# A convolution with residual add: the weights loaded as 16 rows of 9 KB, with four output channels each, and transposed in 36 pieces of 16 columns

## The chip, the cores and the metric

The kernel runs on one core of a Trainium2 chip. The metric is the device time of one execution in microseconds (us). Before the change it is 124.16 us, the median of three runs that lie between 124.1 and 124.16.

The core has the engines PE (matrix products), DVE (vector work), ACT (scalar work, here casts), POOL (here zeros and the identity) and SP (which only issues transfers here). Sixteen DMA engines, shared by all queues, move data between the chip's main memory (HBM) and the on-chip memory (SBUF). The results of PE land in PSUM, which DVE reads. Engines wait for each other through semaphores.

## The reference

A 3 x 3 convolution with padding 1 over 16 images of 64 channels and 64 x 64 pixels, into 64 channels, and then the addition of a residual. Everything is float32.

```python
batch, c_in, h, w, c_out, k = 16, 64, 64, 64, 64, 3
x_pad = np.pad(x, ((0, 0), (0, 0), (pad, pad), (pad, pad)), mode='constant')
for b in range(batch):
    for co in range(c_out):
        for ci in range(c_in):
            for kh in range(k):
                for kw in range(k):
                    output[b, co] += weight[co, ci, kh, kw] * x_pad[b, ci, kh:kh+h, kw:kw+w]
return (output + residual).astype(np.float32)
```

x, the residual and the output are 16.8 MB each, the weights 0.147 MB. All of it crosses the DMA engines once.

## The kernel before

**Transfers.** The images are taken in pairs: two images of 64 channels fill 128 partitions, and a row of a partition is one channel of 4096 pixels, 16 KB. There are eight pairs. SP issues, in this order, for each pair the load of x (`load_x`, line 71, into one of three buffers `xr`) and the load of the residual (`load_ro`, line 74, into a buffer `ro` of its own for each pair). The load of the very first pair of x is moved ahead of the barrier at the start of the program (`to_the_front`). From the fourth pair on, the load of x waits until ACT has read the buffer that it takes (line 123). Then come the stores (line 77): five in the same queue, each waiting for its pair's additions (line 129), and the last three after everything else is done (lines 217 and 218). All these transfers are in one queue, q1, and are worked off in the order of issue by all 16 DMA engines.

**The weights** are loaded by one DMA that ACT issues (line 151, queue q10) into `wraw`. Before the change this is a buffer of 64 partitions, one for each output channel, with a row of 576 float32 numbers (64 input channels times 9 taps), 2304 bytes. PE needs the weights with the input channels on the partitions. So PE waits for the zeros and the identity (line 191) and for the weights (line 192), and then turns the nine 64 x 64 blocks, one for each tap, with a transpose against a 64 x 64 identity (line 195), into the first bank of PSUM. DVE copies the nine blocks from there, cast to bfloat16, into the tile `wl` in six instructions (line 172). `wl` holds each tap in the two places where a 128 x 128 matrix of two output rows and two input rows needs it; the places that stay zero are set by POOL (lines 147 and 148).

**POOL** first makes the identity (a memset on line 133 and a select on line 135), then sets the border rows of the four `xp` buffers and the zero places of `wl`. Each of these counts `s_id` up.

**The loop over 16 images.** ACT casts the even and the odd rows of an image into the two halves of an `xp` buffer (lines 159 and 163). PE runs 24 matrix products of 128 x 128 by some 512 for each image, six weight tiles with four chunks each (lines 83 and 84). It starts the first image when `wl` is written (`s_bank`, line 199) and the image is cast (`s_pack`, line 200). DVE adds the residual to the two halves of the result, in place in `ro` (line 182), and that frees the store. The order on each engine is the order of the program.

Of the kernel before, what the change touches and what calls it, by code (L numbers as in the profile page):

```python
# [8 lines left out]
FP32 = mybir.dt.float32  # L9
# [6 lines left out]
def kernel(  # L16
# [7 lines left out]
    nc = tc.nc  # L24
# [18 lines left out]
    w_flat = weight.rearrange("co ci kh kw -> co (ci kh kw)")  # L43

    pool = ctx.enter_context(tc.tile_pool(name="pool", bufs=1))
    psum = ctx.enter_context(tc.tile_pool(name="psum", bufs=1, space=bass.MemoryType.PSUM))

    ident = pool.tile([64, 64], FP32)
    ro = [pool.tile([128, NPIX], FP32, name=f"ro{p}") for p in range(NPAIR)]
    xr = [nc.alloc_sbuf_tensor(f"xr{i}", [128, NPIX], FP32) for i in range(NXR)]  # L50

    xp = [pool.tile([128, J + 1, W], BF16, name=f"xp{i}") for i in range(NXP)]
    wraw = nc.alloc_sbuf_tensor("wraw", [64, 576], FP32)
    wl = pool.tile([128, 2, 3, 2, 64], BF16)
    ps = [psum.tile([128, NCHUNK, JC, W], FP32, name=f"ps{i}") for i in range(2)]

    sem = lambda name: tc.alloc_semaphore(name)
    s_w = sem("s_w")
# [11 lines left out]
    def load_x(p):  # L70
        return nc.sync.dma_start(out=xr[p % NXR][:, :], in_=x_bc[128 * p : 128 * p + 128, :]).then_inc(s_x[p % NXR], 16)

    def load_ro(p):
        nc.sync.dma_start(out=ro[p][:, :], in_=res_bc[128 * p : 128 * p + 128, :]).then_inc(s_r[p], 16)

    def store(p):
        return nc.sync.dma_start(out=out_bc[128 * p : 128 * p + 128, :], in_=ro[p][:, :])

    def matmul(out_, lhsT, rhs, start, stop, ldweights):

        e = nc.tensor
        if ldweights:
            return e.matmul(out=out_, lhsT=lhsT, rhs=rhs, start=start, stop=stop, skip_group_check=True)  # L83
        return e.add_instruction(  # L84
            mybir.InstMatmult(
                name=nc.get_next_instruction_name(),
                engine=PE,
                ins=[e.lower_ap(rhs), e.lower_ap(lhsT)],
                outs=[e.lower_ap(out_)],
                start_tensor_calc=start,  # L90
                stop_tensor_calc=stop,
                tile_size=(128, 128),
                tile_position=(0, 0),
                bass_skip_group_check=True,
                ldweights=False,
            )
        )

    def to_the_front(dma):

        def fixed(ap):
            t = ap.bass_ap.tensor.name
            return mybir.PhysicalAccessPattern(
                ap=ap.ap, offset=ap.bass_ap.offset, dtype=ap.dtype, memref=t, memsetref=t + "_set", bass_ap=ap.bass_ap
            )

        front = nc.main_func.blocks[0].instructions
        here = nc.cur_bb.bb.instructions  # L110
        ins = here.pop()
        assert ins.name == dma.ins.name
        at = next(
            i for i, e in enumerate(front) if e.engine == mybir.EngineType.SP and isinstance(e, mybir.InstDrain)
        )
        front.insert(at, copy.replace(ins, ins=[fixed(a) for a in ins.ins], outs=[fixed(a) for a in ins.outs]))

    with tc.tile_critical(no_gpsimd_drain=True):  # L118

        for p in range(NPAIR):  # L120
            if p >= NXR:

                nc.sync.wait_ge(s_half, 2 * (p - NXR) + 3)
            i = load_x(p)
            if p == 0:
                to_the_front(i)
            load_ro(p)
        for p in range(NEARLY):
            nc.sync.wait_ge(s_add, 2 * p + 3)
            store(p).then_inc(s_out, 16)  # L130


        nc.gpsimd.memset(ident[:, :], 0.0).then_inc(s_id, 1)  # L133
        nc.gpsimd.wait_ge(s_id, 1)
        nc.gpsimd.affine_select(  # L135
            out=ident[:, :],
            in_=ident[:, :],
            compare_op=mybir.AluOpType.not_equal,
            fill=1.0,
            base=0,  # L140
            pattern=[[-1, 64]],
            channel_multiplier=1,
        ).then_inc(s_id, 1)
        for t in xp:
            nc.gpsimd.memset(t[0:64, 0, :], 0.0).then_inc(s_id, 1)  # L145
            nc.gpsimd.memset(t[64:128, J, :], 0.0).then_inc(s_id, 1)  # L146
        nc.gpsimd.memset(wl[0:64, 0, :, 1, :], 0.0).then_inc(s_id, 1)  # L147
        nc.gpsimd.memset(wl[64:128, 1, :, 0, :], 0.0).then_inc(s_id, 1)  # L148


        nc.scalar.dma_start(out=wraw[:, :], in_=w_flat[:, :]).then_inc(s_w, 16)
        for n in range(B):
            p, im = divmod(n, 2)
            hp = slice(64 * im, 64 * im + 64)
            x4 = xr[p % NXR].rearrange("q (j two w) -> q j two w", two=2, w=W)
            t = xp[n % NXP]
            if im == 0:
                nc.scalar.wait_ge(s_x[p % NXR], 16 * (p // NXR + 1))
            i = nc.scalar.copy(out=t[64:128, 0:J, :], in_=x4[hp, :, 0, :])  # L159
            i.then_inc(s_half, 1)  # L160
            if n >= NXP:
                i._wait_ge(s_conv, n - NXP + 1)
            nc.scalar.copy(out=t[0:64, 1 : J + 1, :], in_=x4[hp, :, 1, :]).then_inc(s_pack, 1)  # L163


        nc.vector.wait_ge(s_wt, 1)
        tpf = ps[0].rearrange("p c j w -> p (c j) w")

        blocks = ((0, 0, 0, 0), (1, 0, 0, 1), (1, 0, 1, 0), (0, 1, 0, 2), (0, 1, 1, 1), (1, 1, 1, 2))
        for half, d, par, kh in blocks:  # L170
            hp = slice(64 * half, 64 * half + 64)
            i = nc.vector.tensor_copy(out=wl[hp, d, :, par, :], in_=tpf[0:64, 3 * kh : 3 * kh + 3, :])  # L172
        i.then_inc(s_bank, 2)
        for n in range(B):
            p, im = divmod(n, 2)
            hp = slice(64 * im, 64 * im + 64)
            o4 = ro[p].rearrange("q (j two w) -> q j two w", two=2, w=W)
            psj = ps[n % 2].rearrange("q c j w -> q (c j) w")
            if im == 0:
                nc.vector.wait_ge(s_r[p], 16)  # L180
            for par in range(2):
                i = nc.vector.tensor_tensor(  # L182
                    out=o4[hp, :, par, :], in0=psj[64 * par : 64 * par + 64, :, :], in1=o4[hp, :, par, :], op=ADD
                )
                if par == 0:
                    i._wait_ge(s_conv, n + 1)

                i.then_inc(s_add if par == 0 or n == B - 1 else s_bank, 1)


        nc.tensor.wait_ge(s_id, 4 + 2 * NXP)
        nc.tensor.wait_ge(s_w, 16)
        wraw3 = wraw.rearrange("p (ci t) -> p ci t", t=9)
        for t in range(9):
            i = nc.tensor.transpose(out=ps[0][0:64, t // 8, t % 8, :], in_=wraw3[:, :, t], identity=ident[:, :])  # L195
        i.then_inc(s_wt, 1)
        with nc.Fori(0, B // NXP, 1, engines=[PE]):
            for n in range(NXP):
                nc.tensor.wait_ge(s_bank, 1).then_inc(s_bank, -1)
                nc.tensor.wait_ge(s_pack, 1).then_inc(s_pack, -1)  # L200
                order = [(1, 0), (1, 1), (0, 0), (0, 1), (2, 0), (2, 1)]
                for i, (kw, d) in enumerate(order):
                    xlo, xhi = max(0, 1 - kw), min(W, W + 1 - kw)
                    for c in range(NCHUNK):
                        j0 = JC * c
                        m = matmul(
                            ps[n % 2][:, c, :, xlo:xhi],
                            wl[:, d, kw, :, :].rearrange("q r c -> q (r c)"),
                            xp[n][:, j0 + d : j0 + d + JC, xlo + kw - 1 : xhi + kw - 1],
                            i == 0,  # L210
                            i == len(order) - 1,
                            c == 0,
                        )
                m.then_inc(s_conv, 1)
# [36 lines left out]
```

## Time and profile before

| what | value |
|---|---|
| median time | 124.16 us |
| the profiled execution's own time | 124.16 us |
| its span, first to last instruction | 122.1 us |
| PE busy | 86.5 us (71%) |
| DVE busy | 75.2 us (62%) |
| ACT busy | 62.0 us (51%) |
| moved by DMA | 50.48 MB, mean 413 GB/s |
| queue q1 (loads and stores) | 97.8% of the 16 DMA engines' time |
| queue q10 (weights) | 0.4%, 80 packets |
| weights: issue to landing | 8.5 us |

In the profile, a line such as L195 is a line of the kernel; `wl<-ps` says which tile is written from which. A group of instructions is shown with its busy time, the mean duration of one, and what ended the idle time before it. A view of windows gives, for each stretch of time, the busy time of each engine and then the clock granted to PE, the share of the 16 DMA engines that was busy, and the rate that they moved. A share can be a little over 1 in a short window, because a packet is counted in the window where it starts. A timeline gives start, duration, engine, line and operation. SPq, ACTq and PEq are the sequencers of these engines, which issue DMAs and wait.

### The profile page before, as it was taken

How to read it: one execution, taken by the hardware profiler on the slowest of the kernel's cores; microseconds unless marked ns; L12 is line 12 of the kernel's file. 1: busy time of each engine (PE TensorE's matmuls, PEld its weight loads, DVE VectorE, ACT ScalarE, POOL GpSimd, SP SyncE). 2: the span in 40 equal slices, each digit the busy share in tenths (PEclk: the TensorE clock that was granted, in tenths of full speed). 3: DMA queues.
4: the chain of work that ended last, by engine and by line, in shares of the span. 5: the costliest groups of instructions: out<-in, count | busy, mean ns of one | idle time of the engine just before them, and what ended most of it. 6: DMA issues, size and time to landing. Idle time of an engine off the chain costs nothing.

```text
span 122.1 us, 729 instructions
## 1 busy us (share of the span) xinstructions
PE 86.5 (71%) x389; PEld 10.4 (9%) x105; DVE 75.2 (62%) x38; ACT 62.0 (51%) x33; POOL 2.2 (2%) x16
## 2 busy tenths in 40 slices
PE   0003799999999999999999999999999930000000
PEld 0003000101111010101010101111110100000000
DVE  0004101989889898898989889898798988000000
ACT  4009948966984993992994896699000000000000
POOL 5100000000000000000000000000000000000000
PEclk9999999999999999999999999999999999555555
DMA  6999999999999999999999999999999999999993
GB/s 182 408 348 429 429 429 429 429 424 429 429 429 424 429 429 429 429 429 429 429 429 419 429 429 424 429 429 429 435 435 435 429 429 429 435 435 429 429 429 140
DMA packets 3536, 50.48 MB, mean 413 GB/s; under 512 B 400, under 2 KB 400, under 8 KB 464
## 3 DMA queue, kind: packets, MB, share of 16 engines
q1 hardware_dynamic: 3456, 50.33, 97.8%
q10 hardware_dynamic: 80, 0.15, 0.4%
HBM read 33.70 MB, written 16.78 MB: 413 GB/s over the span
## 4 chain that ended last, share of the span: by engine, by line
PE 70%; DVEq 2%; DVE 2%; issue 0%
PE ps L84 53%; PE ps L83 17%; DVEq L118 2%; DVE ro L182 2%
## 5 line engine op out<-in xcount | busy, mean ns | idle before, releaser
L182 DVE TENSOR_TENSOR ro<-ps,ro 64x2048 f32<-64x2048 f32 x32 | 73.2, 2289 | 17.4 <-PE ps L84 16.9
L84 PE MATMUL ps<-xp,wl 128*128 128x504 bf16 (+1 forms) x288 | 79.9, 387 | 0.2
L159 ACT CAST xp<-xr 64x2048 bf16<-64x2048 f32 x16 | 30.3, 1896 | 21.3 <-DMA xr<-in_x_dram 21.1
L83 PE MATMUL ps<-xp,wl 128*128 128x504 bf16 (+1 forms) x92 | 35.6, 387 | 2.4 <-PEq L200 2.4
L163 ACT CAST xp<-xr 64x2048 bf16<-64x2048 f32 x16 | 30.4, 1897 | 0.4
L83 PEld LDWEIGHTS ps<-xp,wl 128*128 128x128 bf16 x96 | 9.5, 99 | 77.5 <-issue 77.5
L172 DVE CAST wl<-ps 64x192 bf16<-64x192 f32 x6 | 1.9, 347 | 10.9 <-PE ps L195 10.8
L195 PE MATMUL ps<-ident,wraw 64*64 64x64 f32 x9 | 1.1, 305 | 9.6 <-DMA wraw<-in_weight_dram 9.6
L159 ACT ACT_TABLE_LOAD x1 | 1.3, 1283 | 1.5 <-SPq L118 1.5
L195 PEld LDWEIGHTS ps<-ident,wraw 64*64 64x64 f32 x9 | 0.9, 163 | 9.6 <-issue 9.6
L146 POOL MEMSET xp<- 64x64 bf16 x4 | 0.6, 147 | 0.2
L145 POOL MEMSET xp<- 64x64 bf16 x4 | 0.6, 145 | 0.2
L148 POOL MEMSET wl<- 64x192 bf16 x1 | 0.3, 253 | 0.1
L147 POOL MEMSET wl<- 64x192 bf16 x1 | 0.3, 252 | 0.1
L135 POOL TENSOR_SCALAR_AFFINE_SELECT ident<-ident 64x64 f32<-64x64 f32 x1 | 0.2, 233 | 0.2 <-POOL ident L133 0.2
L133 POOL MEMSET ident<- 64x64 f32 x1 | 0.1, 145 | 0.5 <-SPq L118 0.5
L235 POOL MEMSET const-bfloat16-1.0<- 128x1 bf16 x1 | 0.1, 113 | 0.0
L235 POOL MEMSET const-uint8-127<- 128x1 uint8 x1 | 0.1, 112 | 0.0
L235 POOL MEMSET const-float32-1.0<- 128x1 f32 x1 | 0.1, 109 | 0.0
L235 POOL MEMSET const-float32-0.0<- 128x1 f32 x1 | 0.1, 104 | 0.2 <-issue 0.2
## 6 DMA issues: line engine op xcount, KB each, us to landing
xr<-in_x_dram SPq DMA_DIRECT2D x8, 2048.0 KB, 17.6
ro<-in_residual_dram SPq DMA_DIRECT2D x8, 2048.0 KB, 22.1
out_dram<-ro SPq DMA_DIRECT2D x8, 2048.0 KB, 28.7
wraw<-in_weight_dram ACTq DMA_DIRECT2D x1, 144.0 KB, 8.5
```

Source lines behind the costliest of these rows:

```text
L83: return e.matmul(out=out_, lhsT=lhsT, rhs=rhs, start=start, stop=stop, skip_group_check=True)
L84: return e.add_instruction(mybir.InstMatmult(name=nc.get_next_instruction_name(), engine=PE, ins=[e.lower_ap(rhs), e.lower_ap(lhsT)], outs ...
L118: with tc.tile_critical(no_gpsimd_drain=True):
L145: nc.gpsimd.memset(t[0:64, 0, :], 0.0).then_inc(s_id, 1)
L146: nc.gpsimd.memset(t[64:128, J, :], 0.0).then_inc(s_id, 1)
L147: nc.gpsimd.memset(wl[0:64, 0, :, 1, :], 0.0).then_inc(s_id, 1)
L159: i = nc.scalar.copy(out=t[64:128, 0:J, :], in_=x4[hp, :, 0, :])
L163: nc.scalar.copy(out=t[0:64, 1 : J + 1, :], in_=x4[hp, :, 1, :]).then_inc(s_pack, 1)
L172: i = nc.vector.tensor_copy(out=wl[hp, d, :, par, :], in_=tpf[0:64, 3 * kh : 3 * kh + 3, :])
L182: i = nc.vector.tensor_tensor(out=o4[hp, :, par, :], in0=psj[64 * par : 64 * par + 64, :, :], in1=o4[hp, :, par, :], op=ADD)
L195: i = nc.tensor.transpose(out=ps[0][0:64, t // 8, t % 8, :], in_=wraw3[:, :, t], identity=ident[:, :])
L235: nc = _bacc.Bacc("TRN2", target_bir_lowering=False, num_devices=1)
```

## The change

The same bytes of the weights are read as 16 rows of 9216 bytes: a row holds four output channels that follow each other in memory. `wraw` so has 16 partitions, and partition q holds the output channels 4q to 4q + 3. A transpose takes, for one tap t and one u from 0 to 3, the 16 x 64 block of the output channels 4q + u, and writes 64 x 16 into every fourth column of the block of that tap in PSUM. There are 36 of them in place of nine. The identity is 16 x 16. What lies in PSUM afterwards is the same, and DVE's six copies, PE's loop and everything else are as before.

```diff
-    ident = pool.tile([64, 64], FP32)
+    ident = pool.tile([16, 16], FP32)
...
-    wraw = nc.alloc_sbuf_tensor("wraw", [64, 576], FP32)
+    wraw = nc.alloc_sbuf_tensor("wraw", [16, 4, 576], FP32)
...
-            pattern=[[-1, 64]],
+            pattern=[[-1, 16]],
...
-        nc.scalar.dma_start(out=wraw[:, :], in_=w_flat[:, :]).then_inc(s_w, 16)
+        nc.scalar.dma_start(out=wraw[:, :, :], in_=w_flat.rearrange("(q u) f -> q u f", u=4)).then_inc(s_w, 16)
...
-        wraw3 = wraw.rearrange("p (ci t) -> p ci t", t=9)
+        wraw4 = wraw.rearrange("q u (ci t) -> q u t ci", t=9)
         for t in range(9):
-            i = nc.tensor.transpose(out=ps[0][0:64, t // 8, t % 8, :], in_=wraw3[:, :, t], identity=ident[:, :])
+            for u in range(4):
+                i = nc.tensor.transpose(
+                    out=ps[0].rearrange("p c j (q u) -> p (c j) u q", u=4)[0:64, t, u, :],
+                    in_=wraw4[:, u, t, :],
+                    identity=ident[:, :],
+                )
         i.then_inc(s_wt, 1)
```

## The prediction

> **What bounds the kernel now.** I read the page first, for the shares; then windows of the DMA, because the page shows it full; then the timeline of the first 14 us, where the change lies, and of the end. The span is 122.1 us, the profiled execution took 124.16 us, which is also the median of the three runs, so every sum below is made on 124.16 with 2.06 us lying around the span.
>
> Lines of the page:
>
> ```profile
> span 122.1 us, 729 instructions
> ...
> PE 86.5 (71%) x389; PEld 10.4 (9%) x105; DVE 75.2 (62%) x38; ACT 62.0 (51%) x33; POOL 2.2 (2%) x16
> ...
> DMA  6999999999999999999999999999999999999993
> ...
> q1 hardware_dynamic: 3456, 50.33, 97.8%
> q10 hardware_dynamic: 80, 0.15, 0.4%
> ```
>
> No engine is above 71%, but the 16 DMA engines are full from the second slice to the last but one: q1 alone (the loads and stores that SP issues) takes 97.8% of them. The bytes set the time: 50.48 MB at some 429 GB/s are 117.7 us. The chain that ended last names PE for 70%, since it follows semaphores and does not know that the queue behind the last stores is still full. So I ask of everything whether it delays the DMA stream, and of the compute chain only whether the last stores are issued late enough for the stream to run dry. q10 is the weight load: 80 packets, 0.15 MB.
>
> Windows of the DMA (the last two columns are the share of the 16 engines and GB/s):
>
> ```profile
> 5.00:6.25 1.25, 0.00 (x0) 0.00 (x0) 0.00 (x0) 0.00 (x0) 0.00 (x0) 1.00 1.12 441
> 6.25:8.65 2.40, 0.00 (x0) 0.00 (x0) 0.00 (x0) 0.00 (x0) 0.00 (x0) 1.00 0.97 323
> 8.65:12.00 3.35, 1.14 (x9) 0.93 (x9) 1.16 (x4) 3.08 (x2) 0.00 (x0) 1.00 1.00 425
> ...
> 30.00:100.00 70.00, 68.58 (x316) 7.70 (x79) 61.51 (x28) 44.08 (x24) 0.00 (x0) 1.00 1.01 429
> ```
>
> There is one weak stretch: from 6.25 to 8.65 us the engines are busy (0.97) and move only 323 GB/s; before and after it the rate is full. The packet records of the trace put the 64 weight packets of 2304 B at 5.2 to 8.3 us, so the stretch begins about 1 us after the first and ends 0.4 us after the last. The large packets running in it are longer too, on all 16 engines, also those whose weight packets are done.
>
> The start and the end, from the timeline and from windows:
>
> ```profile
> 0.95 0.53 ACTq L151 DMA_DIRECT2D wraw<-in_weight_dram  x1
> ...
> 9.60 0.93 PEld L195 LDWEIGHTS ps<-ident,wraw 64*64 64x64 f32 x9 [9.60 <-issue]
> 9.63 1.14 PE L195 MATMUL ps<-ident,wraw 64*64 64x64 f32 x9 [9.63 <-DMA wraw<-in_weight_dram]
> 10.81 1.97 DVE L172 CAST wl<-ps 64x192 bf16<-64x192 f32 x6 [10.81 <-PE ps L195]
> 10.81 1.90 ACT L163 CAST xp<-xr 64x2048 bf16<-64x2048 f32 x1
> ...
> 13.12 0.58 PE L83 MATMUL ps<-xp,wl 128*128 128x512 bf16 x1 [2.35 <-PEq L200]
> ```
>
> ```profile
> 98.78 4.61 DVE L182 TENSOR_TENSOR ro<-ps,ro 64x2048 f32<-64x2048 f32 x2 [0.58 <-PE ps L84]
> 103.68 1.76 SPq L77 DMA_DIRECT2D out_dram<-ro  x3
> ```
>
> ```profile
> 105.00:105.50 0.50, 0.00 (x0) 0.00 (x0) 0.00 (x0) 0.00 (x0) 0.00 (x0) 0.50 1.00 426
> 105.50:106.00 0.50, 0.00 (x0) 0.00 (x0) 0.00 (x0) 0.00 (x0) 0.00 (x0) 0.50 1.16 492
> ...
> 120.00:120.50 0.50, 0.00 (x0) 0.00 (x0) 0.00 (x0) 0.00 (x0) 0.00 (x0) 0.50 0.16 66
> ```
>
> Weights landed, nine transposes, six copies into wl: they end at 12.78 us. The casts of the first image end at 12.71. PE needs both and starts at 13.12; from there to 98.7 it has no gap. The last three stores are issued at 103.68. Their 6.29 MB take 14.6 us at 430 GB/s, and the DMA stops at about 120.1, so their bytes started at about 105.4, with no dip at 105 to 106. The very first load was issued at 0.00 and its bytes came from about 1.0 us on. The same latency would have let the stores begin at 104.7. So the compute chain may slip by about 0.7 us before the stream runs dry. Bounds of this cover: 0, if the latency is the whole 1.7 us, and 1.7 us.
>
> **The change part by part.**
>
> **POOL.** Identity of 16 x 16 in place of 64 x 64: the memset (0.14 us) and the select (0.23 us) can only shrink. POOL ends its zeros at 3.71 us and PE waits for the weights until 9.60, so this is worth nothing; the cover is 5.9 us.
>
> **Queues.** No wait is added and nothing is moved past a queue. SP's issues stay. ACT still issues one DMA (0.53 us) ahead of its table load, which ends at 2.80, and ACT then waits for x until 8.89. A shorter issue gains nothing, and one of twice the length is hidden.
>
> **The weight transfer** is what touches the bound. Now: over 5.00 to 8.65 us the windows give (1.25 x 441 + 2.40 x 323) / 3.65 = 363 GB/s against 429, which is 0.24 MB or 0.56 us lost; the weights' own 0.147 MB are 0.34 us. The load costs the stream 0.90 us today, 0.56 of it over its bytes. Afterwards the bytes are the same, in 16 rows that land in 16 partitions in place of 64. If the loss went with the number of packets, it would fall to a quarter: 0.14 + 0.34 = 0.48, a gain of 0.42 us; if nothing were lost, the gain is 0.56. If it goes with what each receiving partition has to take, it rises up to four times: 2.24 + 0.34 = 2.58, a loss of 1.68 us. I stand nearer to the second, because the slow stretch does not look like a price per packet: it starts late, ends late, and slows the x packets on every engine, like a backlog on the receiving side. Between none and four times I take twice: 1.12 + 0.34 = 1.46, that is +0.56 us. Both ends stay for the range.
>
> [...]
>
> **The transposes.** Nine at a pitch of (1.14 - 0.29) / 8 = 0.107 us become 36. Each still loads 64 columns as its stationary side; the moving side shrinks from 64 columns to 16. Bounds of the pitch: a quarter (0.027, 1.2 us in all with the 0.29 us tail) if the moving columns set it, and unchanged (0.107, 4.0 us) if the load does. I take between them 0.067, 2.6 us in all, against 1.14 now: +1.5 us.
>
> [...]
>
> Against this the weights may land earlier. One packet and one completion for each engine, instead of four packets with a large one between each two (about 0.7 to 0.9 us apart in the packet records), saves up to 2 us: 7.6 instead of 9.6. With the backlog that I expect, about 1 us: 8.6. Transposes end at 8.6 + 2.6 = 11.2, 0.4 us later than 10.77. The six copies and PE's start follow by as much: 13.5. This is inside the 0.7 us. Should it go well (7.6 + 1.2 = 8.8), the casts at 12.71 take over and PE starts 0.1 to 0.2 us earlier, worth nothing since the DMA sets the end.
>
> **Sum.** POOL 0, issue 0, transfer +0.56 (-0.56 to +1.68), transposes 0 behind the cover: 124.16 + 0.56 = 124.72, said as 124.7.
>
> **The rivals.**
>
> *Per-packet cost (faster).* A quarter of the packets means a quarter of the loss: -0.42, 123.74; down to 123.6 if nothing is lost. For it: packets of 2304 B are the only small data packets in the trace, and the weak stretch lies where they are. Against it: the first of them ran at 0.093 us each with the rate still full (441 GB/s at 5.00 to 6.25). It decides if the loss follows packets, not partitions.
>
> *No difference.* The weak stretch has another cause (first reads of the residual tensor come in the same microseconds), or the AP is still cut into pieces of 2304 B and the change does not do what it says, or the two effects cancel: 124.0 to 124.4. Against the first: no other start of a load shows a weak stretch.
>
> *PE becomes late (slower).* If the weights land at 9.6 as now and the pitch stays 0.107, the transposes end at 13.6, 2.9 us later; less the 0.7 of cover, 2.2 us of idle DMA: 126.4. It decides from an end of the transposes after about 11.5 us. Against it: fewer packets cannot well land later than now unless the backlog is severe, and the moving side is a quarter.
>
> **How the numbers follow.** A measurement of this kernel can tell about 0.2% (0.25 us) from no change. Transfer dearer, my forecast: 0.45, with loss factors 1.5 to 3, so 124.4 to 125.3. PE late: 0.10, 125.0 to 126.4. No difference: 0.18. Faster: 0.27, 123.6 to 123.9. So slower 0.55, same 0.18, faster 0.27. The range 123.65 to 125.25 leaves out most of the late PE, and little of the ends of the other two, some 0.15 in all.
>
> **What would show it.** Right: q10 with 32 packets; a window between 5 and 9 us with the engines busy and a rate below 323 GB/s, or as weak for longer; the last three stores' bytes without a dip, the DMA ending near 120.7. The landing of wraw near 7.5 us after its issue; transposes of 2 to 3 us. Wrong: the rate between 6 and 9 us near 400, and a DMA that ends before 119.9 (per-packet cost); a window below 400 GB/s between 104 and 108 us (PE late).

## The result and the profile after

The changed kernel takes 125.87 us (median of six runs, 125.14 to 126.04) against 124.18 us before (124.1 to 124.43, six runs). The ratio is 1.0123 with an interval of 1.0096 to 1.0150. It is slower by 1.7 us, 1.4%. The way was forecast; the size was not, and the time lies above the range.

The two profiled executions split this in two. Inside the span, the changed kernel is 1.0 us longer. Outside the span, the profiled execution has 126.01 - 123.1 = 2.9 us in place of 2.06, and the six runs of the changed kernel have 2.3 to 2.9 us. Both parts need a cause.

From the page of the changed kernel:

```profile
span 123.1 us, 779 instructions
...
q1 hardware_dynamic: 3456, 50.33, 97.5%
q10 hardware_dynamic: 32, 0.15, 0.5%
```

The weights now come in 32 packets (16 of data, 16 completions) instead of 80, and they take more of the DMA engines' time, not less. The windows, with the share of the DMA engines and GB/s in the last two columns:

```profile
5.00:6.25 1.25, 0.00 (x0) 0.00 (x0) 0.00 (x0) 0.00 (x0) 0.00 (x0) 1.00 1.44 276
6.25:8.65 2.40, 0.00 (x0) 0.00 (x0) 0.00 (x0) 0.00 (x0) 0.00 (x0) 1.00 0.80 241
8.65:12.00 3.35, 2.27 (x36) 2.19 (x36) 0.17 (x1) 1.96 (x2) 0.00 (x0) 1.00 1.01 430
30.00:100.00 70.00, 68.28 (x311) 7.68 (x79) 61.50 (x28) 45.18 (x24) 0.00 (x0) 1.00 1.01 429
```

The weak stretch is deeper and starts earlier. Over 5.00 to 8.65 us the rate was 364 GB/s and is now 253; against 429 that is a loss of (429 - 253) x 3.65 / 429 = 1.50 us, where it was 0.55. The difference, 0.95 us, is nearly all of the growth of the span (1.0 us). After 8.65 us the rate is as before.

The timeline of the changed kernel, first the start, then the end:

```profile
0.96 0.40 ACTq L151 DMA_DIRECT2D wraw<-in_weight_dram  x1
...
9.49 2.19 PEld L196 LDWEIGHTS ps<-ident,wraw 16*64 16x64 f32 x36 [9.49 <-issue]
9.53 2.27 PE L196 MATMUL ps<-ident,wraw 16*64 16x16 f32 x36 [9.53 <-DMA wraw<-in_weight_dram]
10.02 1.90 ACT L159 CAST xp<-xr 64x2048 bf16<-64x2048 f32 x1 [7.36 <-DMA xr<-in_x_dram]
11.83 1.97 DVE L172 CAST wl<-ps 64x192 bf16<-64x192 f32 x6 [11.83 <-PE ps L196]
...
14.10 0.59 PE L83 MATMUL ps<-xp,wl 128*128 128x512 bf16 x1 [2.30 <-PEq L205]
...
17.01 0.10 PEld L83 LDWEIGHTS ps<-xp,wl 128*128 128x128 bf16 x1 [1.52 <-issue]
17.22 0.38 PE L83 MATMUL ps<-xp,wl 128*128 128x504 bf16 x1
```

```profile
98.68 4.61 DVE L182 TENSOR_TENSOR ro<-ps,ro 64x2048 f32<-64x2048 f32 x2 [0.58 <-PE ps L84]
103.58 1.51 SPq L77 DMA_DIRECT2D out_dram<-ro  x3
```

The weights land when they did before (9.5 us against 9.6), the first x lands 1.1 us later (10.0 against 8.9), and PE starts its loop 1.0 us later (14.10 against 13.12). Yet the last stores are issued at 103.58, against 103.68 before. PE's products fall from 0.63 to 0.38 us at 17.2 us in this execution, and before the change only at 18.2 us:

```profile
16.49 0.63 PE L83 MATMUL ps<-xp,wl 128*128 128x504 bf16 x1
...
18.18 0.38 PE L83 MATMUL ps<-xp,wl 128*128 128x504 bf16 x1
```

So PE made up for its late start. The compute chain costs nothing here: between 103 and 108 us the rate is 436 GB/s, without a dip. The DMA stream itself is late. By the packet records its last packet ends at 121.85 us, against 120.75 before.

### The profile page after: what moved, and what is told of

The parts are those of the page before. It is cut to its first block, busy times and chain, and to the rows that moved or that the text cites. A ratio compares the mean times of both kernels' runs of the same rounds, so it can differ in the third digit from the quotient of the medians.

```text
span 123.1 us, 779 instructions
## 1 busy us (share of the span) xinstructions
PE 86.4 (70%) x412; PEld 11.6 (9%) x132; DVE 75.2 (61%) x38; ACT 62.0 (50%) x33; POOL 2.1 (2%) x16
## 4 chain that ended last, share of the span: by engine, by line
PE 68%; DVEq 2%; DVE 2%; issue 0%
PE ps L84 52%; PE ps L83 17%; DVEq L118 2%; DVE ro L182 2%
## 5 line engine op out<-in xcount | busy, mean ns | idle before, releaser
L84 PE MATMUL ps<-xp,wl 128*128 128x504 bf16 (+1 forms) x284 | 78.8, 384 | 0.4
L83 PE MATMUL ps<-xp,wl 128*128 128x504 bf16 (+1 forms) x92 | 35.4, 385 | 2.3 <-PEq L205 2.3
L196 PE MATMUL ps<-ident,wraw 16*64 16x16 f32 x36 | 2.3, 214 | 9.5 <-DMA wraw<-in_weight_dram 9.5
L196 PEld LDWEIGHTS ps<-ident,wraw 16*64 16x64 f32 x36 | 2.2, 149 | 9.5 <-issue 9.5
```

Of the source, the lines that this page charges most:

```text
L84: return e.add_instruction(mybir.InstMatmult(name=nc.get_next_instruction_name(), engine=PE, ins=[e.lower_ap(rhs), e.lower_ap(lhsT)], outs ...
L196: i = nc.tensor.transpose(out=ps[0].rearrange("p c j (q u) -> p (c j) u q", u=4)[0:64, t, u, :], in_=wraw4[:, u, t, :], identity=ident[:, :],)
```

## The experiments

Three questions were open: whether the landing of the rows or the transposes made the span longer; if the landing, by which property of it; and what the extra time outside the span is. All spans and times of a run are from that run's own executions.

**Nine transposes with the 16 rows.** On top of the changed kernel:

```diff
+        nc.vector.memset(ps[0].rearrange("p c j w -> p (c j) w")[0:64, 0:9, :], 0.0).then_inc(s_z, 1)
...
-            for u in range(4):
+            for u in range(1):
```

> The changed kernel with nine transposes in place of 36: the 27 with u above 0 are left out, and DVE writes zeros to that part of PSUM early, so three quarters of the weights are zero in the output. The transfer of the weights is untouched. Changed against before: span 123.1 against 122.1 us, and 2.9 against 2.06 us outside the span. Theory: the landing of the 16 rows alone makes the span longer, and the 54 extra instructions of PE alone make the time outside the span longer. Then: rate at 5.00 to 8.65 us as low as in the changed kernel, span 123.1 (0.15 either way), time 125.2. Rival for the span (late PE): transposes end 1 us earlier, span back to 122.1 to 122.4. Rival for the time outside: it comes with the transfer, then time 125.9.

125.28 us, ratio 1.0097 (1.0070 to 1.0124); span 123.0 to 123.5, 2.2 to 2.3 us outside it. The window and the transposes:

```profile
5.00:8.65 3.65, 0.00 (x0) 0.00 (x0) 0.00 (x0) 0.00 (x0) 0.00 (x0) 1.00 1.02 222
...
9.45 0.68 PE L199 MATMUL ps<-ident,wraw 16*64 16x16 f32 x9 [9.45 <-DMA wraw<-in_weight_dram]
```

The span is that of the changed kernel although the transposes end at 10.1 us, earlier than before the change. So the transfer alone makes the span longer, and the transposes have no part in it. The time outside the span is nearly back to that of before, so the 27 transposes have a part in that, some 0.5 us of the median of 2.7.

**The same 16 rows on spread partitions.** On top of the changed kernel; the weights are not used in it:

```diff
+    wspread = nc.alloc_sbuf_tensor("wspread", [128, 4, 576], FP32)
+    wraw = nc.alloc_sbuf_tensor("wraw", [16, 64], FP32)
...
-        nc.scalar.dma_start(out=wraw[:, :, :], in_=w_flat.rearrange("(q u) f -> q u f", u=4)).then_inc(s_w, 16)
+        nc.scalar.dma_start(out=wspread[0:128:8, :, :], in_=w_flat.rearrange("(q u) f -> q u f", u=4)).then_inc(s_w, 16)
```

> The changed kernel's DMA with the same 16 rows of 9 KB, but landing on every eighth partition (0, 8, ... 120) in place of 0 to 15. The transposes read a tile of zeros instead, so the convolution is left out of the output; PE, DVE and ACT issue the same instructions as in the changed kernel. [...] Rivals (number of partitions; length of a row or a packet): both unchanged, span 123.1. Time outside the span as in the changed kernel, 2.9 us, if PE instructions make it.

Spans of 122.0 to 122.5 us, and 2.5 to 3.4 us outside (time 125.37, ratio 1.0099, 1.0073 to 1.0126).

```profile
5.00:8.65 3.65, 0.25 (x5) 0.28 (x6) 0.00 (x0) 0.00 (x0) 0.00 (x0) 1.00 1.00 352
8.65:12.00 3.35, 1.82 (x35) 1.71 (x33) 1.47 (x5) 3.08 (x2) 0.00 (x0) 1.00 1.02 435
```

This is the run that decides. Rows, packets, bytes and the number of partitions are those of the changed kernel; only where the 16 partitions lie is different. The rate in the weak stretch rises from 253 to 352 GB/s, the loss falls from 1.50 to 0.66 us, and most of the growth of the span is gone. So neither the length of a row nor the number of partitions makes the larger part of the loss. The time is still 1.2 us above before, because the time outside the span stays long.

**32 rows.** On top of the changed kernel: `wraw` of `[32, 2, 576]`, `u=2`, an identity of 32 x 32, 18 transposes. The number of partitions and the length of a row both lie between those of the two kernels.

> The changed kernel with 32 rows of 4608 bytes, two output channels each, and 18 transposes of 32 columns. [...] Time outside the span: between 2.06 and 2.9 us, by the number of PE instructions.

123.92 us, ratio 0.9979 (0.9965 to 0.9993), spans of 121.5 to 122.2.

```profile
5.00:8.65 3.65, 0.00 (x0) 0.00 (x0) 0.00 (x0) 0.00 (x0) 0.00 (x0) 1.00 1.01 359
30.00:100.00 70.00, 68.60 (x316) 7.70 (x79) 61.50 (x28) 43.94 (x24) 0.00 (x0) 1.00 1.01 431
```

The weak stretch is as weak as with 64 rows (359 against 364 GB/s), with half the packets and half the partitions, so the loss does not follow the number of partitions or the length of a row here. But the kernel is a little faster than before, and for another reason: the loads run at 431 GB/s between 30 and 100 us instead of 429. The smaller identity had moved the residual buffers to other addresses; whether that is the reason is tested below.

**128 rows.** On top of the kernel before; the rate in question is the one at 5.00 to 8.65 us:

```diff
-    wraw = nc.alloc_sbuf_tensor("wraw", [64, 576], FP32)
+    wraw = nc.alloc_sbuf_tensor("wraw", [128, 288], FP32)
...
-        nc.scalar.dma_start(out=wraw[:, :], in_=w_flat[:, :]).then_inc(s_w, 16)
+        nc.scalar.dma_start(out=wraw[:, :], in_=w_flat.rearrange("co (h f) -> (co h) f", h=2)).then_inc(s_w, 16)
...
+            for h in range(2):
+                i = nc.tensor.matmul(
+                    out=ps[0][32 * h : 32 * h + 32, t // 8, t % 8, :],
+                    lhsT=wraw3[:, :, t],
+                    rhs=ident.rearrange("p (c h) -> p h c", h=2)[:, h, :],
...
```

> 128 rows of 1152 bytes, half an output channel each, on all 128 partitions, turned in 18 products of a 128 x 32 block with every second column of a 128 x 128 identity. [...] Rival (more and smaller packets cost more): rate 340 or less, span 122.3 or more. [...]

124.67 us (median of twelve executions, 124.25 to 126.18), ratio 1.0037 (1.0020 to 1.0054). The first window shows what became of the weak stretch; the landing and the last window say why the time did not follow it. They are from an execution of 125.42 us:

```profile
5.00:8.65 3.65, 0.00 (x0) 0.00 (x0) 0.00 (x0) 0.73 (x1) 0.00 (x0) 1.00 1.01 427
...
11.16 2.14 PE L197 MATMUL ps<-ident,wraw 128*32 128x64 f32 x36 [11.16 <-DMA wraw<-in_weight_dram]
...
103.00:108.00 5.00, 0.00 (x0) 0.00 (x0) 3.04 (x2) 0.00 (x0) 0.00 (x0) 0.84 0.56 239
```

The weak stretch is gone: 427 GB/s, although there are twice as many packets, and smaller ones, than before the change. Part of them come after 8.65 us, but from there to 12 us the rate is 425. The packet records agree: every large packet that starts between 5.00 and 8.65 us takes 611 ns, where some took 922 ns before and 1674 ns in the changed kernel. But each engine now has eight small packets, each with a large one of x between, so the weights land at 11.1 us in place of 9.6. PE starts at 15.60, the last stores are issued at 106.36, and the stream runs dry: 239 GB/s between 103 and 108 us, over 2 us lost in this execution. Here the third rival of the prediction came true, in another kernel.

The rates fall into three levels: with the rows on partitions 0 to 15, 253 GB/s in the changed kernel; on 0 to 31, on 0 to 63, and on every eighth, 352 to 364; on all 128, 427. The loss at these levels is 1.50, 0.55 to 0.66 and 0.0 us. So it goes with where the rows land, and what makes the three levels is not shown.

**64 rows over all partitions.** The four packets per engine of before, landing on `wraw[0:128:2]`, with nine products and aligned buffers. The rate in question is again the one at 5.00 to 8.65 us.

> The kernel before with the same 64 rows of 2304 bytes, but landing on every second of the 128 partitions (DVE first writes zeros to the whole buffer, and ACT's issue waits for that, some 1 us), turned by nine products with every second column of a 128 x 128 identity; and with the buffers at multiples of 256 bytes as in the aligned run (123.58 us). [...] Rival (number or size of packets): rate 373 as in the aligned run, 123.6.

123.67 us, ratio 0.9956 (0.9936 to 0.9975).

```profile
5.00:8.65 3.65, 0.00 (x0) 0.00 (x0) 0.00 (x0) 0.56 (x1) 0.00 (x0) 1.00 1.07 453
103.00:108.00 5.00, 0.00 (x0) 0.00 (x0) 1.36 (x1) 0.00 (x0) 0.00 (x0) 0.66 0.85 357
```

The weak stretch is gone again (from 8.65 to 12 us the rate is 406, so it is some 430 over both), every large packet of these 3.65 us takes 611 ns, and the weights land at 9.3 us. The time is still that of the aligned run (123.58 us), although the loss at the start is gone: the nine products over 128 rows take 2.41 us, PE starts 1.2 us later than in the aligned run, and the stores, issued at 104.66 for a stream that is now ready sooner, meet a dry stream. What the transfer gave, the chain took back.

**36 transposes with the transfer of before.** On top of the kernel before, `for _ in range(4):` around each of the nine transposes.

> The kernel before with its 64 rows of weights, and each of the nine transposes issued four times over: 36 transposes after PE's wait for the weights, as many PE instructions there as in the changed kernel, with the transfer of before. At a pitch of 0.107 us they end at 13.6, 2.9 us later than before. Theory (the transfer makes the span longer, the transposes do not): rate at 5.00 to 8.65 us as before (364 GB/s). [...] Rival (the chain has more cover, 1.7 us or above): span 122.1 to 123.3. Time outside the span: 2.9 us if as many PE instructions behind the wait make it, 2.1 if not.

The four executions are widely spread: 124.36, 124.63, 125.80 and 126.40 us (ratio 1.0116, 1.0069 to 1.0163). The spans are 122.3 to 123.7, and outside them are 2.0 to 2.1 us in three executions and 3.6 in the slowest. In the profiled execution, with a span of 122.3:

```profile
5.00:8.65 3.65, 0.00 (x0) 0.00 (x0) 0.00 (x0) 0.00 (x0) 0.00 (x0) 1.00 1.03 377
103.00:108.00 5.00, 0.00 (x0) 0.00 (x0) 1.94 (x1) 0.00 (x0) 0.00 (x0) 0.61 0.92 390
```

The start has no deeper weak stretch. PE begins 2.5 us late (15.60), the stores are issued 1.56 us late (105.24), and the dip is (429 - 390) x 5 / 429 = 0.45 us. So the cover of the compute chain is some 1.1 us in that execution, between the 0.7 and the 1.7 of the prediction.

**More PE code with the transfer of before.** 27 and 54 transposes of the identity, ahead of PE's wait for the weights:

```diff
+        for _ in range(27):
+            nc.tensor.transpose(out=ps[1][0:64, 0, 0, :], in_=ident[:, :], identity=ident[:, :])
         nc.tensor.wait_ge(s_w, 16)
```

> The kernel before, with 27 more transposes on PE (of the identity, into a part of PSUM that is written over later), ahead of its wait for the weights: as many PE instructions as the changed kernel has, at a time when PE idles. Theory (the number of PE instructions makes the time outside the span longer): span 122.1, time 124.16 + 0.75 = 124.9. Rival (it does not): span 122.1, time 124.2.

> The kernel before with 54 more small transposes of the identity ahead of PE's wait for the weights, where PE idles: 108 more PE instructions, twice as many as the change adds. Theory (the number of PE instructions makes the time outside the span longer): every execution has 2.5 to 2.9 us outside the span, time 124.9. Rival (only what stands behind the wait counts, or nothing of it): 2.1 us outside, time 124.2. The span stays at 122.1 by both.

With 27: 124.26 us, ratio 1.0006 (0.9990 to 1.0022); 2.0 to 2.1 us outside the span in eight executions, 2.5 and 2.7 in two. This is a miss: with as many PE instructions as the changed kernel, the time outside rose only now and then. With 54: 125.1 us, ratio 1.0052 (1.0029 to 1.0076), but not as expected: the time outside is 2.0 to 2.3 us, and the spans fall into two groups, 121.9 to 122.3 and 123.0 to 123.3. The DMA view of that run has a line that no run with fewer instructions has inside its span:

```profile
q1 hardware_dynamic: 3456, 50.33, 97.0%
q10 hardware_dynamic: 80, 0.15, 0.4%
q8 instruction: 1, 0.02, 0.1%
```

One packet of 16 KB, of a queue that carries instructions. The packet records put it at 33.8 us and give it 1.07 us on its engine. The last two packets of the stream then end at 121.39 and 122.00 us, one after the other, when all others have ended by 120.81: it looks as if one engine alone were late and ended the stream. Only this execution has records, so that the packet makes the upper group of spans is likely, not shown. In the records of the changed kernel and of the run with spread rows, such a packet is there too, but it starts 1.9 and 1.8 us after the end of the span. It ends 3.1 and 2.7 us after it, and these executions have 2.9 and 2.5 us outside their spans, so the time outside goes with it. No other profiled execution has it, and three of them have as many PE instructions as the changed kernel (27 more, 36 with the transfer of before, 128 rows).

**More PE code in the changed kernel.** The same 27 transposes on top of the changed kernel, 63 in all.

> The changed kernel with 27 more transposes of the identity, into a part of PSUM that is written over later, ahead of PE's wait for the weights: 63 in all, as in the run in which a packet of the instruction queue showed up at 33.8 us. Theory (the time outside the span in the changed kernel is a fetch of PE's code that falls at the end of the program; with still more code it falls into the run): outside the span 2.0 to 2.3 us in every execution, the page shows one packet of an instruction queue inside the span, span 123.1 to 124.3. Rival (it comes with the transfer of 16 rows): 2.9 us outside.

125.98 us, ratio 1.0127 (1.0095 to 1.0159); 2.0 to 2.4 us outside, spans of 123.0 to 124.0. The DMA view:

```profile
q1 hardware_dynamic: 3456, 50.33, 96.9%
q10 hardware_dynamic: 32, 0.15, 0.6%
q8 instruction: 1, 0.02, 0.1%
```

As expected, in three executions of four: with still more code the packet moves into the run (30.2 us), the extra time outside the span goes, and the span is up to 0.9 us longer instead. So a fetch of instructions fits the 0.6 us outside the span. It is not shown that the longer PE program alone brings it. With 16 rows and 36 transposes, all ten executions (changed kernel and spread rows) have 2.3 us or more outside. With as many PE instructions and other transfers it is two of ten, one of four, and with 128 rows none of twelve (2.0 to 2.1). With 16 rows and nine transposes, all four have 2.2 to 2.3. So the 27 further transposes are needed, something in the kernels with 16 rows makes the fetch come nearly always, and what that is stays open.

**The start address.** On top of the kernel before:

```diff
+    nc.alloc_sbuf_tensor("pad", [128, 32], FP32)
     xr = [nc.alloc_sbuf_tensor(f"xr{i}", [128, NPIX], FP32) for i in range(NXR)]
```

> The kernel before with 128 unused bytes ahead of the buffers, so that the x and residual buffers start at a multiple of 256 bytes in their partitions. In the run with 32 rows the residual buffers were moved to such a start and the loads ran at 431 GB/s between 30 and 100 us, against 429. Theory (the start address made that): 431 GB/s, span 121.7, time 123.8. Rival (it came with the weight transfer, or from one execution to the next): 429 GB/s, span 122.1, time 124.2.

123.58 us, ratio 0.9956 (0.9942 to 0.9969), spans of 121.3 to 121.7.

```profile
30.00:100.00 70.00, 68.43 (x315) 7.62 (x79) 61.50 (x28) 43.64 (x24) 0.00 (x0) 1.00 1.01 431
```

128 unused bytes make the kernel 0.6 us faster than before. This version beats both kernels, and it is made without the change. The changed kernel's smaller identity moves its residual buffers too, but its loads ran at 429 GB/s as before, so the address has no part in its loss.

> The run with 32 rows (123.92 us), with all x and residual buffers at multiples of 256 bytes. Theory: 32 rows cost what 64 cost (0.6 to 0.7 us over 3 to 12 us), so this equals the aligned kernel with 64 rows: 123.6. Rival (32 rows are cheaper than 64, apart from the start address): 123.3 or less.

123.71 us, ratio 0.9953 (0.9933 to 0.9973); seven executions lie between 123.52 and 123.84, an eighth took 134.21. With aligned buffers, 32 rows and 64 rows are equal, and the small gain of the 32 rows was that of the address.

## Why the prediction was wrong

*What bounds the kernel.* Right. The DMA stream set the end in both kernels, and a late PE start of 1.0 us cost nothing.

*The transfer.* The side was right, the unit and the size were not. The prediction took the loss over the weights' bytes as twice the 0.56 us; it was 1.50 us, 2.7 times. The term was +0.56 and measured +0.95. That the weak stretch lies on the receiving side, and is not a price per packet, held: the run with the same 16 packets on spread partitions settles it (352 GB/s in place of 253). But the prediction put it down to what each receiving partition has to take, and that failed. With 32 rows each partition takes twice as much as with 64, and the loss is the same (0.60 and 0.55 us); with 16 spread rows it takes as much as in the changed kernel, and the loss is 0.66 in place of 1.50. What counts is where the partitions lie. The factor of two was a middle between none and four, so that it came near was in part luck.

*The landing.* Wrong. One packet per engine was to land the weights at 8.6 us; they landed at 9.5. The packet records show why: packets of 9216 B took 0.35 us in the first instants and up to 1.1 us then, and the large packets beside them up to 1.7 us. The last packet of the weights ended at 7.7 us, and the last completion came at 8.9. On spread partitions they landed at 8.4.

*The transposes.* The pitch taken was 0.067 us; it is (2.27 - 0.21) / 35 = 0.059, and the whole 2.3 us against 2.6. The quarter pitch (0.027) was not had.

*The cover.* Transposes ended 1.0 us later, more than the 0.7 us that was counted as cover, at no cost. That was luck, as far as the sum goes: the products of 0.38 us began earlier in that execution (17.2 us against 18.2), so the last stores were not late at all. The cover itself is larger, some 1.1 us in the run that measured it.

*The time around the span.* This is the step that failed outright, and the one that took the time out of the range: the transfer's +0.95 alone would have given 125.1. The sum was made with "2.06 us lying around the span" as a constant. It grew to a median of 2.7 us, which is 0.6 of the 1.7 us. A fetch of instructions behind the end goes with it; it needs the 27 further transposes, and why it came in nearly every execution of this kernel stays open. The prediction counted these transposes by their time on PE alone and never as code. Span +1.0 and around it +0.6 come within 0.1 of the measured +1.7.

*The rivals.* Per-packet cost and no difference are ruled out by the runs with spread rows and with 128 rows. PE becoming late did not decide here, but it did with 128 rows, where more packets per engine brought the weights later.

## What to carry to other kernels

The DMA stream was the bound here, and the small transfer was paid by where it landed, not only by its bytes and packets: the same 144 KB cost the stream 1.5 us more than their bytes on partitions 0 to 15, 0.6 us on 0 to 63 or spread by eights, and nothing on all 128. The opposite pull was that 128 rows meant eight packets per engine among those of x in place of four, and a landing at 11.1 us in place of 9.6, so ask in another kernel which of the two the next stage waits for. And an unrolled helper stage is also code: look for packets of an instruction queue (one of 16 KB here, 1.07 us in the run with 54 more transposes), and compare the time outside the span as well as the span.

## What the runs showed of the hardware that was not expected

A packet of 16 KB on an instruction queue can fall into the run: it did so in the two longest programs (832 and 840 instructions against 729 before), and behind the span in two of the five with 778 to 780. In the run with 54 more transposes it held one DMA engine for 1.07 us, and the spans of these two programs were up to 1.2 and 0.9 us longer than without the further transposes.

Moving the x and residual buffers by 128 unused bytes took the loads from 429 GB/s to 431 over 70 us (0.5%), and the kernel 0.6 us down. A packet of a load took 614.7 ns on average between 12 and 78 us, and 611.0 with the moved buffers; a packet of a store took 611 ns in both. Why the start of a buffer counts for the loads and not for the stores is not shown.

The moment at which PE's products fall from 0.63 to 0.38 us is not fixed to its own start: it came at 18.2 us after a start at 13.1, and at 17.2 us after a start at 14.1. That is why, in that execution, a start 1 us later did not end later. The granted clock is 1.00 before and after that moment in both kernels, and what makes the products shorter is not shown.
